# Decay matrices of a gated-delta layer: one symmetric matrix with masks applied later, in place of two masked ones

## The chip, the cores and the metric

The kernel runs on one core of a Trainium2 chip. The metric is the device time of one execution in microseconds. Engine names in the profile: PE is TensorE (matmuls; PEld its weight loads), DVE is VectorE, ACT is ScalarE, POOL is GpSimd, SP is SyncE, whose queue issues most loads; the ACT queue issues DMAs too. SBUF is the on-chip memory, PSUM the banks into which TensorE writes.

## What is computed

Two layers of a streaming encoder over 1024 prompt frames and 64 sample frames, 1024 features, in float32. The first layer (gated convolution and band attention) is not touched. The second is a gated DeltaNet with 8 heads of 128 keys and values, worked through in chunks of 64 frames. Cut to what matters here:

```python
gc = jnp.cumsum(g, axis=1)            # g <= 0: log decays, 64 frames of a chunk
decay = jnp.exp(jnp.where(incl, gct[..., :, None] - gct[..., None, :], -jnp.inf))
a = jnp.where(strict, bt[..., :, None] * kk * decay, 0.0)     # kk = k k^T
tmat = a + jnp.eye(L)
sol = lax.linalg.triangular_solve(tmat, rhs, left_side=True, lower=True, unit_diagonal=True)
qk = jnp.einsum('blhd,bmhd->bhlm', q, k) * decay
o = (q * exp(gc)) @ S + qk @ u
S_new = exp(g_last) * S + k_dec^T @ u
```

So for each chunk and head a 64 x 64 matrix exp(gc_i - gc_j) is needed twice: below the diagonal (i > j) for the triangular system, and with the diagonal, transposed, for the product of queries and keys.

## The kernel before, in words

**Order of the work.** TensorE's instructions are emitted in an order that `Order` (L75) keeps: generators yield the nanoseconds after which they want to go on, `mm` and `tr` (L115, L121) advance a clock by the estimated length of each matmul, and the free generator of the lowest rank goes next. Ranks: a scan 1, `solve` 1.3, `join` 1.5, `substitute` 1.6, `prepare` 2, the gates 2, the decays 3, and 5 for `main`, which is the stream of projections that fills what the others leave. The order on the other engines is made by the compiler's scheduler from what is ready in its own estimate of time; each engine then runs its queue in order.

**Layer two.** 17 chunks of 64 frames in batches of 6, 6 and 5 (`BATCHES`, L31); heads go in pairs, two heads by 64 rows on the 128 partitions, four pairs. `odd` (L670) first projects the keys and queries of pair 0 in three groups of frames (L1141 on), each with a short convolution on ScalarE and VectorE (`conv`, L701: an activation that evacuates the PSUM bank, L708, products with shifted copies, L721, and a tanh or SiLU, L724 to L727; pair 0 uses tanh). In the last group it adds `gates` (L779), which makes the sums gc and their exponentials, and `decays` (L819). Then come pair 0's values and the other pairs' keys, queries and values (L1165 on). Weights come through SP (L157) and are split into a high part by ScalarE (L163) and a low part by VectorE (L164).

**The decays before.** For each of four pairs and three batches: VectorE makes gx, a diagonal matrix of gc (L832); a matmul with a block of ones spreads it over the rows, into a PSUM bank with the tag `tr`; VectorE subtracts gc (L836) into an SBUF buffer df; GpSimd twice adds a mask of zeros and -1e30 (L839), each time into a buffer of its own; ScalarE takes the exponentials (L840) and the ACT queue stores each to DRAM (L841). All four buffers (gx, df, two results) are parts of `buf`, one of each. A name `dec{p}` is marked done after a pair's three batches.

**The batches.** `prepare` (L853) of a pair's batch waits for `dec{p}`, loads both matrices (L867, L868, SP queue, one buffer each), transposes keys and queries in `tr` banks, sums their squares on ScalarE (L882), makes reciprocal roots in small steps on VectorE (`rsqrt`, L683, its last step L690), scales the keys kt by kap on GpSimd (L894), and multiplies products of keys and queries in PSUM by scale and decay: An (L903) below the diagonal, KQD (L904) above it. Af (L907 to L910) gathers the 16-column blocks on An's diagonal; they go through DRAM to `substitute` (L916), which inverts them on GpSimd (L928, L929). `join` (L936) puts the inverse together, `solve` (L1004) applies it and `scan` (L1030) runs the recurrence. `add_pair` (L1124) names what each waits for: `prepare` of batch n for the one of n-1, the solve of n-2 and the scan of n-3. The tag `tr` has two PSUM banks for all of these (`pst`, L677).

Of the kernel before, what the change touches and what calls it, by code (L numbers as in the profile page):

```python
# [7 lines left out]
F32 = mybir.dt.float32  # L8
F32R = mybir.dt.float32r
I32 = mybir.dt.int32  # L10
AF = mybir.ActivationFunctionType
ALU = mybir.AluOpType
# [3 lines left out]
P = 128  # L16
# [8 lines left out]
NCH = T // 64  # L25
SCH = NCH - 1
EPS = 1e-6
NEG = -1.0e30
# [8 lines left out]

C_ID, C_U, C_BD = 0, 128, 256
C_ID64 = 384
C_M1, C_M2 = 448, 512  # L40
C_B16 = 576
C_H16 = 580
C_H = 582
# [13 lines left out]
def constants():  # L57
    c = np.zeros((P, NCONST), np.float32)
    p = np.arange(P)
    h, i = p // 64, p % 64  # L60
    same = h[:, None] == h[None, :]
    c[:, C_ID:C_ID + P] = np.eye(P)
    c[:, C_U:C_U + P] = same & (i[:, None] <= i[None, :])
    c[:, C_BD:C_BD + P] = same
    c[:, C_H:C_H + 2] = h[:, None] == np.arange(2)[None, :]
    j = np.arange(64)
    c[:, C_ID64:C_ID64 + 64] = i[:, None] == j[None, :]
    c[:, C_M1:C_M1 + 64] = np.where(j[None, :] < i[:, None], 0.0, NEG)
    c[:, C_M2:C_M2 + 64] = np.where(j[None, :] >= i[:, None], 0.0, NEG)
    c[:, C_B16:C_B16 + 4] = (i // 16)[:, None] == np.arange(4)[None, :]  # L70
    c[:, C_H16:C_H16 + 2] = (i // 16 % 2)[:, None] == np.arange(2)[None, :]
    return c
# [35 lines left out]
class Net:  # L108
# [120 lines left out]
    def run(self):  # L229
        nc, tc, I, O = self.nc, self.tc, self.I, self.O  # L230
        self.opened = {}
        const, self.wp, self.hp = self.open("const"), self.open("wp"), self.open("hp")
        dram = self.open("dram", space=DRAM)
        with tc.tile_pool(name="pj", bufs=2, space=PSUM) as self.pj:
            self.cst = const.tile([P, NCONST], F32, name="cst")
            self.par = const.tile([P, NPAR], F32, name="par")
            self.eps = const.tile([P, 1], F32, name="eps")
            self.cwa = const.tile([P, 12], F32, name="cwa")
            self.cwh = const.tile([P, 3, 8], F32, name="cwh")
            mean = const.tile([P, 1], F32, name="mean")  # L240
            self.dve.memset(mean, 1.0 / D)
            self.meanm = mean.broadcast_to([P, P])
            self.dve.memset(self.eps, EPS)
            self.ident = self.cst[:, C_ID:C_ID + P]
            self.mixd = [dram.tile([P, KT, T], F32, name=f"mixd{l}") for l in range(2)]
            self.od = dram.tile([P, KT, T], F32, name="od")
            self.xd = dram.tile([P, KT, T], F32, name="xd")
            self.Ld = dram.tile([8, LROW], F32, name="Ld")
            self.Gd = [dram.tile([P, LROW], F32, name=f"Gd{h}") for h in range(8)]
            self.Dd = [dram.tile([P, NCH, 64], F32, name=f"Dd{i}") for i in range(8)]  # L250
            self.Sd = [[dram.tile([m, P, 16], F32, name=f"Sd{a}{b}") for b, (c0, m) in enumerate(BATCHES)] for a in range(2)]
            self.H = [None] * len(GROUPS)
            self.ready, self.held = [], 0
            self.queue = []
            for p in range(4):
                self.queue += [I["w_in0"][i + p] for i in (24, 16, 20, 28, 4, 8, 12, 0)]
            self.queue += [I["w_out0"][m] for g in GROUPS for m in range(KT)]
            for p in range(4):
                self.queue += [I["w_in1"][i + 2 * p] for i in (8, 9, 0, 1, 16, 17)]
            self.queue += [I["w_in1"][24 + i] for i in range(8)]  # L260
            self.queue += [I["w_out1"][m] for g in GROUPS for m in range(KT)]
            self.banks, self.pg = [self.pj], None
            self.order.add("main", 5, self.main())
            self.order.run()
            self.close(*reversed([n for n in self.opened]))
# [404 lines left out]
    def odd(self):  # L670
        nc, tc, I, O = self.nc, self.tc, self.I, self.O
        act, dve, pool, par, cst = self.act, self.dve, self.pool, self.par, self.cst
        w_in, mix, order, Dd, od, Sd = I["w_in1"], self.mixd[1], self.order, self.Dd, self.od, self.Sd
# [3 lines left out]
        def pst(tag):  # L677
            return self.pg.tile([P, 512], F32, name=tag, tag=tag, bufs=2 if tag in ("tr", "su") else 1)
# [100 lines left out]
        def gates(ba):  # L779
# [36 lines left out]
            act.activation(egl.rearrange("p q a c -> p (q a c)"), ps[:, 136:272], AF.Exp)  # L816
            yield 1500

        def decays():  # L819
            gc = G["gc"]  # L820
            buf = G["buf"]

            def part(i, m):
                return buf[:, 384 * i:384 * i + 64 * m].rearrange("p (c j) -> p c j", j=64)

            for p in range(4):
                yield 0
                for c0, m in BATCHES:
                    sh = [P, m, 64]
                    gcb = gc[:, p, c0:c0 + m].unsqueeze(2).broadcast_to(sh)  # L830
                    gx, df = part(0, m), part(1, m)
                    dve.tensor_tensor(gx, gcb, cst[:, C_ID64:C_ID64 + 64].unsqueeze(1).broadcast_to(sh), ALU.mult)  # L832
                    yield 900
                    ps = pst("tr")
                    self.mm(ps[:, :64 * m], cst[:, C_BD:C_BD + P], gx.rearrange("p c j -> p (c j)"))
                    dve.tensor_tensor(df, ps[:, :64 * m].rearrange("p (c j) -> p c j", j=64), gcb, ALU.subtract)  # L836
                    for q, (cm, op) in enumerate(((C_M1, ALU.subtract), (C_M2, ALU.add))):
                        dx = part(2 + q, m)
                        pool.tensor_tensor(dx, cst[:, cm:cm + 64].unsqueeze(1).broadcast_to(sh), df, op)  # L839
                        act.activation(dx, dx, AF.Exp)  # L840
                        nc.scalar.dma_start(Dd[2 * p + q][:, c0:c0 + m, :], dx)  # L841
                    yield 2500
                order.done.add(f"dec{p}")

# [8 lines left out]
        def prepare(p, b):  # L853
            c0, nb = BATCHES[b]
            kq = KQ[p]
            n = NB * p + b
            yield 4000 if b == 0 else 0
            beta, egc, dec = G["beta"], G["egc"], G["dec"]

            def bt(name, w, bufs=1):  # L860
                return self.kp.tile([P, NBM, w], F32, name=name, tag=name, bufs=bufs)[:, :nb, :]
# [1 line left out]
            def small(name):  # L863
                return self.kp.tile([P, NBM], F32, name=name, tag=name, bufs=3)[:, :nb]

            Dst, DT = bt("Dst", 64), bt("DT", 64)
            nc.sync.dma_start(Dst, Dd[2 * p][:, c0:c0 + nb, :])  # L867
            nc.sync.dma_start(DT, Dd[2 * p + 1][:, c0:c0 + nb, :])  # L868
            kd, kt = bt("kd", P, 3), bt("kt", P, 2)
            ss = self.kp.tile([P, 2, NBM], F32, name="ss", tag="ss", bufs=2)[:, :, :nb]  # L870
            rr = self.kp.tile([P, 2, NBM], F32, name="rr", tag="rr", bufs=3)[:, :, :nb]
# [20 lines left out]
            dve.scalar_tensor_tensor(sA, sT, -1.0, rr[:, 0, :], ALU.mult, ALU.mult)  # L892
            dve.scalar_tensor_tensor(kap, egc[:, p, c0:c0 + nb], -1.0, rr[:, 0, :], ALU.mult, ALU.mult)
            pool.tensor_tensor(kt, kt, kap.unsqueeze(2).broadcast_to([P, nb, P]), ALU.mult)  # L894
            An, KQD = bt("An", 64, 2), bt("KQD", 64, 3)
            for i0 in range(0, nb, 4):
                m = min(4, nb - i0)
                ps = pst("tr").rearrange("p (c j) -> p c j", j=P)
                for i in range(m):
                    for q in range(2):  # L900
                        self.mm(ps[64 * q:64 * q + 64, i, :], kq[:, 0, c0 + i0 + i, q, :], kq[:, :, c0 + i0 + i, q, :], share=1.6)
                for i in range(m):
                    dve.scalar_tensor_tensor(An[:, i0 + i, :], ps[:, i, 0:64], sA[:, i0 + i:i0 + i + 1], Dst[:, i0 + i, :], ALU.mult, ALU.mult)  # L903
                dve.tensor_tensor(KQD[:, i0:i0 + m, :], ps[:, :m, 64:128], DT[:, i0:i0 + m, :], ALU.mult)  # L904
                yield 510

            Af = bt("Af", 16)  # L907
            dve.tensor_scalar(Af, An[:, :, 0:16], cst[:, C_B16:C_B16 + 1], None, ALU.mult)
            for j in range(1, 4):
                dve.scalar_tensor_tensor(Af, An[:, :, 16 * j:16 * j + 16], cst[:, C_B16 + j:C_B16 + j + 1], Af, ALU.mult, ALU.add)  # L910
            sa = Sd[0][b]
            nc.sync.dma_start(sa.rearrange("c r j -> r c j"), Af)
            R[p, b] = dict(kd=kd, kt=kt, KQD=KQD, rq=rr[:, 1, :], An=An, sT=sT)
# [210 lines left out]
        def add_pair(p):  # L1124
            for b in range(NB):
                n = NB * p + b
                def after(name, i):
                    return [f"{name}{i}"] if i >= 0 else []

                order.add(f"scan{n}", 1, scan(p, b), [f"wy{n}"] + after("scan", n - 1))  # L1130
                order.add(f"wy{n}", 1.3, solve(p, b), [f"inv{n}", f"v{p}"])
                order.add(f"inv{n}", 1.5, join(p, b), [f"sub{n}"] + after("wy", n - 1))
                order.add(f"sub{n}", 1.6, substitute(p, b), [f"prep{n}"] + after("sub", n - 1))
                order.add(f"prep{n}", 2, prepare(p, b), [f"dec{p}"] + after("prep", n - 1) + after("wy", n - 2) + after("scan", n - 3))

        new_kq(0)
        ba = k1.tile([P, 4 * T], F32, name="ba", tag="kq", bufs=2)[0:16, 0:T]
# [133 lines left out]
```

## Time and profile before

| | us |
|---|---|
| median of 3 runs | 1475.85 (1473.38 to 1477.38) |
| the profiled execution, its own time | 1476.87 |
| its span, first to last instruction | 1475.1 |
| mean granted TensorE clock | 0.980 |
| the twelve decay batches, first gx to last store issued | 714.1 to 797.2 |
| first state update to last of layer two | 815.5 to 1313.1 |

The profile is of one execution. Busy times are sums of instruction durations; matmul durations overlap. "Idle before" is an engine's idle time ahead of an instruction, put down to what released it last. A granted clock below 1 means that TensorE ran slower than its full rate in that window. A tile's name stands for all its buffers; `dbuf` is the `buf` of the gates and decays.

### The profile page before, as it was taken

What the parts mean: (1) busy time and instruction counts of PE and PEld (TensorE: products, weight loads), DVE (VectorE), ACT (ScalarE), POOL (GpSimd) and SP (SyncE); (2) the same over time, 40 slices, a digit from 0 to 9 for tenths busy, and PEclk for the clock granted to TensorE, in tenths of its full rate; (3) what the DMA queues carried; (4) which work ended last, traced back from release to release, by engine and by line L of the source; (5) the groups of instructions that cost most, each with busy time, mean ns of one, the idle gap of its engine ahead of it and who ended that gap; (6) DMA issues with size and microseconds to landing.
All of it is one profiled execution on the core that took longest, in us unless ns stands there. A gap on an engine that the chain in (4) does not pass through costs nothing. (4 is left out here: it accounts for less than half of the span.)

```text
span 1475.1 us, 28417 instructions
## 1 busy us (share of the span) xinstructions
PE 1371.8 (93%) x10578; PEld 1233.6 (84%) x10578; DVE 884.4 (60%) x2496; ACT 681.4 (46%) x1780; POOL 314.3 (21%) x813
## 2 busy tenths in 40 slices
PE   4999999999999999989878999999999989998995
PEld 3888998999899899878867777878887877888985
DVE  6647237425624855768687767666766656443654
ACT  6544144234424446775455553544443534323642
POOL 4100000000000012341136224240424152210332
PEclk9999999999999999999999999999999999999998
DMA  5231210211121164551432222122211232347454
GB/s 204 63 136 44 78 59 26 78 61 45 53 70 58 34 216 137 181 186 60 85 98 69 40 43 61 35 42 48 70 33 41 61 87 70 92 122 229 150 188 157
DMA packets 114378, 133.12 MB, mean 90 GB/s; under 512 B 35568, under 2 KB 81336, under 8 KB 114240
## 3 DMA queue, kind: packets, MB, share of 16 engines
q1 hardware_dynamic: 82128, 101.86, 24.2%
q10 hardware_dynamic: 32112, 29.45, 6.1%
q8 instruction: 83, 1.36, 0.4%
q14 instruction: 55, 0.45, 0.1%
HBM read 99.91 MB, written 34.51 MB: 91 GB/s over the span
## 5 line engine op out<-in xcount | busy, mean ns | idle before, releaser
L119 PE MATMUL pjt<-hhi,wlo 128*128 128x384 f32 (+1 forms) x1768 | 620.8, 351 | 2.5 <-DVE wlo L164 2.4
L119 PE MATMUL pjt<-hhi,whi 128*128 128x384 f32 (+1 forms) x1768 | 586.7, 332 | 19.5 <-ACT whi L163 4.1
L119 PE MATMUL pjt<-hlo,whi 128*128 128x384 f32 (+1 forms) x1768 | 585.9, 331 | 7.3 <-DVE hlo L217 6.6
L119 PEld LDWEIGHTS pjt<-hhi,whi 128*128 128x128 f32 x1768 | 339.5, 192 | 29.5 <-ACT hhi L216 6.6
L119 PEld LDWEIGHTS pjt<-hhi,wlo 128*128 128x128 f32 x1768 | 339.9, 192 | 27.5 <-issue 12.4
L119 PEld LDWEIGHTS pjt<-hlo,whi 128*128 128x128 f32 x1768 | 338.4, 191 | 10.5 <-DVE hlo L217 8.8
L164 DVE TENSOR_TENSOR wlo<-wf,whi 128x512 fp32r<-128x512 f32 x222 | 155.8, 727 | 144.7 <-ACT whi L163 143.0
L163 ACT CAST whi<-wf 128x512 fp32r<-128x512 f32 x222 | 130.0, 619 | 160.5 <-PE pjt L119 113.0
L546 ACT ACTIVATE pr<-pr,mx 128x640 f32<-128x640 f32 (+5 forms) x72 | 50.9, 707 | 92.7 <-DVE mx L545 92.2
L721 DVE SCALAR_TENSOR_TENSOR kq<-pjt,par,kq 128x384 f32<-128x384 f32 (+2 forms) x144 | 71.6, 497 | 2.9
L347 POOL TENSOR_TENSOR sqa<-sqa,sq 128x384 f32<-128x384 f32 (+1 forms) x36 | 37.9, 1052 | 154.0 <-ACT sq L345 153.9
L507 POOL MEMSET bias<- 64x64 f32 x8 | 1.4, 178 | 313.1 <-DMA bias<-Gd 312.6
L543 DVE CUSTOM_DVE_ANT_0 pr<-sc,bias 128x640 f32<-128x640 f32 (+5 forms) x72 | 48.0, 666 | 26.3 <-PE sc L119 22.8
L928 POOL TENSOR_TENSOR px<-AL 48x14 f32<-48x14 f32 (+6 forms) x168 | 45.1, 269 | 61.3 <-DMA AL<-Sd 52.2
L1091 DVE SCALAR_TENSOR_TENSOR S<-S,egl,su 128x128 f32<-128x128 f32 x128 | 40.6, 343 | 28.9 <-PE su L119 28.5
L692 POOL TENSOR_TENSOR so<-so 128x4 f32<-128x4 f32 (+2 forms) x72 | 16.8, 233 | 176.7 <-DVE so L685 117.9
L882 ACT ACTIVATE junk<-tr 128x128 f32<-128x128 f32 x136 | 37.7, 277 | 34.9 <-PE tr L124 29.5
L929 POOL TENSOR_TENSOR AL<-AL,px 48x14 f32<-48x14 f32 (+6 forms) x168 | 46.7, 278 | 9.4
L119 PE MATMUL pjt<-mhi,whi 128*128 128x384 f32 x128 | 43.9, 343 | 4.9 <-ACT mhi L163 4.9
L124 PE MATMUL pt<-cst,pr 128*128 128x128 f32 (+1 forms) x280 | 43.2, 269 | 4.4 <-DVE pr L548 2.9
L1050 ACT ACTIVATE junk<-o 128x128 f32<-128x128 f32 x68 | 21.0, 309 | 51.9 <-DVE o L1046 43.1
L119 PE MATMUL pjt<-mlo,whi 128*128 128x384 f32 x128 | 43.9, 343 | 0.0
(238 smaller groups left out, 2208.5 us busy)
## 6 DMA issues: line engine op xcount, KB each, us to landing
wf<-in_w_in SPq DMA_DIRECT2D x128, 256.0 KB, 3.3
wf<-in_w_out SPq DMA_DIRECT2D x96, 256.0 KB, 3.3
mf<-mixd SPq DMA_DIRECT2D x32, 192.0 KB, 3.2
x<-in_x SPq DMA_DIRECT2D x8, 384.0 KB, 5.4
xg<-in_x SPq DMA_DIRECT2D x2, 1536.0 KB
xd<-xg SPq DMA_DIRECT2D x2, 1536.0 KB, 6.9
Dd<-dbuf ACTq DMA_DIRECT2D x16, 192.0 KB, 2.7
od<-o ACTq DMA_DIRECT2D x12, 256.0 KB, 3.4
```

The source lines that it names most:

```text
L119: return self.pe.matmul(out, lhsT=lhsT, rhs=rhs, start=start, stop=stop, **k)
L124: return self.pe.transpose(out, in_, self.ident[0:k, 0:k])
L163: self.act.copy(out=hi, in_=x)
L164: (eng or self.dve).tensor_tensor(lo, x, hi.bitcast(F32), ALU.subtract)
L347: pool.tensor_tensor(acc, acc, sq, ALU.add)
L543: dve.tensor_tensor_reduce(out=cut(pr[0:nq, :nk]), in0=sc[0:nq, :nk // nw, :nw], in1=cut(b["bias"][a][0:nq, j0:j0 + nk]), scale=1.0, scala ...
L546: act.activation(pr[0:nq, :nk], pr[0:nq, :nk], AF.Exp, bias=mx[0:nq, 1:2], scale=1.0, accum_out=mx[0:nq, 2:3])
L721: dve.scalar_tensor_tensor(oi, ch(ps[:, i0 + j + 1:i0 + j + 1 + m]), cw[j], oi, ALU.mult, ALU.add)
L882: act.activation(junk, ps[:, i, :], AF.Square, accum_out=ss[:, a, i0 + i:i0 + i + 1])
L928: pool.tensor_tensor(t, AL[:, j + 1:16, j:j + 1].broadcast_to([lanes, m, w]), x.broadcast_to([lanes, m, w]), ALU.mult)
L929: pool.tensor_tensor(o, o, t, ALU.add)
L1091: dve.scalar_tensor_tensor(Sn[:, q, :], S[:, q, :], egl[:, q, p, c:c + 1], su[q], ALU.mult, ALU.add)
```

## The change

One exponential of minus the absolute difference, exp(-|gc_i - gc_j|), is symmetric; it is kept without a mask, as E. The masks become products later: the upper one (with the diagonal) is multiplied with E into KQD's buffer on GpSimd before KQD's product; the lower one isn't applied to An at all but, strict and inside the 16-column blocks only, to Af. The constants `C_M1` and `C_M2` become `C_LOW` (16 columns of ones below the diagonal of each block) and `C_UP`. The absolute value and the exponential both run on ScalarE, the first out of the PSUM bank, in which VectorE now subtracts in place.

`decays` does pairs 1 to 3 only, with two buffers for gx and three for E, and stores one matrix for each batch. Pair 0's decays are made inside `prepare`, straight into E, with An's buffer as scratch for gx; its batches no longer wait for `dec0` but for the gates. The 4000 ns ahead of a pair's first batch now come after the load or the decay.

```diff
@@ constants
-    c[:, C_M1:C_M1 + 64] = np.where(j[None, :] < i[:, None], 0.0, NEG)
-    c[:, C_M2:C_M2 + 64] = np.where(j[None, :] >= i[:, None], 0.0, NEG)
+    c[:, C_LOW:C_LOW + 16] = j[None, :16] < (i % 16)[:, None]
+    c[:, C_UP:C_UP + 64] = j[None, :] >= i[:, None]
@@ odd
+        def decay(e, gx, p, c0, m):
+            sh = [P, m, 64]
+            gcb = G["gc"][:, p, c0:c0 + m].unsqueeze(2).broadcast_to(sh)
+            dve.tensor_tensor(gx, gcb, cst[:, C_ID64:C_ID64 + 64].unsqueeze(1).broadcast_to(sh), ALU.mult)
+            yield 900
+            ps = pst("tr")[:, :64 * m]
+            self.mm(ps, cst[:, C_BD:C_BD + P], gx.rearrange("p c j -> p (c j)"))
+            ps = ps.rearrange("p (c j) -> p c j", j=64)
+            dve.tensor_tensor(ps, ps, gcb, ALU.subtract)
+            act.activation(e, ps, AF.Abs)
+            act.activation(e, e, AF.Exp, scale=-1.0)
...
-            for p in range(4):
-                yield 0
+            for p in range(1, 4):
                 for c0, m in BATCHES:
...
-                    dve.tensor_tensor(df, ps[:, :64 * m].rearrange("p (c j) -> p c j", j=64), gcb, ALU.subtract)
-                    for q, (cm, op) in enumerate(((C_M1, ALU.subtract), (C_M2, ALU.add))):
-                        dx = part(2 + q, m)
-                        pool.tensor_tensor(dx, cst[:, cm:cm + 64].unsqueeze(1).broadcast_to(sh), df, op)
-                        act.activation(dx, dx, AF.Exp)
-                        nc.scalar.dma_start(Dd[2 * p + q][:, c0:c0 + m, :], dx)
+                    e = piece(2 + i % 3, m)
+                    yield from decay(e, piece(i % 2, m), p, c0, m)
+                    nc.scalar.dma_start(Dd[p][:, c0:c0 + m, :], e)
+                    i += 1
                     yield 2500
@@ prepare
-            yield 4000 if b == 0 else 0
...
-            Dst, DT = bt("Dst", 64), bt("DT", 64)
-            nc.sync.dma_start(Dst, Dd[2 * p][:, c0:c0 + nb, :])
-            nc.sync.dma_start(DT, Dd[2 * p + 1][:, c0:c0 + nb, :])
+            E, An, KQD = bt("E", 64), bt("An", 64, 2), bt("KQD", 64, 3)
+            if p:
+                nc.sync.dma_start(E, Dd[p][:, c0:c0 + nb, :])
+            else:
+                yield from decay(E, An, p, c0, nb)
+            if b == 0:
+                yield 4000
...
             pool.tensor_tensor(kt, kt, kap.unsqueeze(2).broadcast_to([P, nb, P]), ALU.mult)
-            An, KQD = bt("An", 64, 2), bt("KQD", 64, 3)
+            pool.tensor_tensor(KQD, E, cst[:, C_UP:C_UP + 64].unsqueeze(1).broadcast_to([P, nb, 64]), ALU.mult)
...
-                    dve.scalar_tensor_tensor(An[:, i0 + i, :], ps[:, i, 0:64], sA[:, i0 + i:i0 + i + 1], Dst[:, i0 + i, :], ALU.mult, ALU.mult)
-                dve.tensor_tensor(KQD[:, i0:i0 + m, :], ps[:, :m, 64:128], DT[:, i0:i0 + m, :], ALU.mult)
+                    dve.scalar_tensor_tensor(An[:, i0 + i, :], ps[:, i, 0:64], sA[:, i0 + i:i0 + i + 1], E[:, i0 + i, :], ALU.mult, ALU.mult)
+                dve.tensor_tensor(KQD[:, i0:i0 + m, :], ps[:, :m, 64:128], KQD[:, i0:i0 + m, :], ALU.mult)
...
+            dve.tensor_tensor(Af, Af, cst[:, C_LOW:C_LOW + 16].unsqueeze(1).broadcast_to([P, nb, 16]), ALU.mult)
@@ add_pair
-                order.add(f"prep{n}", 2, prepare(p, b), [f"dec{p}"] + after("prep", n - 1) + after("wy", n - 2) + after("scan", n - 3))
+                order.add(f"prep{n}", 2, prepare(p, b), [f"dec{p}" if p else "gates"] + after("prep", n - 1) + after("wy", n - 2) + after("scan", n - 3))
```

More of the change, by code (lines that the diff above doesn't have):

```diff
@@ L39 @@
 C_ID64 = 384
-C_M1, C_M2 = 448, 512
+C_LOW, C_UP = 448, 512
 C_B16 = 576
@@ L249, in run @@
             self.Gd = [dram.tile([P, LROW], F32, name=f"Gd{h}") for h in range(8)]
-            self.Dd = [dram.tile([P, NCH, 64], F32, name=f"Dd{i}") for i in range(8)]
+            self.Dd = [dram.tile([P, NCH, 64], F32, name=f"Dd{i}") for i in range(4)]
             self.Sd = [[dram.tile([m, P, 16], F32, name=f"Sd{a}{b}") for b, (c0, m) in enumerate(BATCHES)] for a in range(2)]
@@ L817, in gates, with piece @@
             yield 1500
+        def decay(e, gx, p, c0, m):
[9 more added lines that the diff above has]
+            act.activation(e, e, AF.Exp, scale=-1.0)
         def decays():
-            gc = G["gc"]
-            buf = G["buf"]
-            def part(i, m):
+            buf, i = G["buf"], 0
+            def piece(i, m):
                 return buf[:, 384 * i:384 * i + 64 * m].rearrange("p (c j) -> p c j", j=64)
-            for p in range(4):
-                yield 0
+            for p in range(1, 4):
                 for c0, m in BATCHES:
[L829 to L836, printed above, removed]
-                    for q, (cm, op) in enumerate(((C_M1, ALU.subtract), (C_M2, ALU.add))):
-                        dx = part(2 + q, m)
-                        pool.tensor_tensor(dx, cst[:, cm:cm + 64].unsqueeze(1).broadcast_to(sh), df, op)
-                        act.activation(dx, dx, AF.Exp)
-                        nc.scalar.dma_start(Dd[2 * p + q][:, c0:c0 + m, :], dx)
+                    e = piece(2 + i % 3, m)
+                    yield from decay(e, piece(i % 2, m), p, c0, m)
+                    nc.scalar.dma_start(Dd[p][:, c0:c0 + m, :], e)
+                    i += 1
                     yield 2500
```

## Prediction

> **What bounds the kernel now.** I began with the page's first part and then asked the view by windows for the stages around the change (columns: window, its length, then busy time and instruction count of PE, PEld, DVE, ACT and POOL, granted clock, DMA share, GB/s).
>
> ```profile
> PE 1371.8 (93%) x10578; PEld 1233.6 (84%) x10578; DVE 884.4 (60%) x2496; ACT 681.4 (46%) x1780; POOL 314.3 (21%) x813
> ```
>
> ```profile
> 713.00:800.00 87.00, 69.92 (x454) 61.14 (x456) 69.56 (x178) 43.90 (x122) 39.86 (x67) 0.90 0.39 96
> 800.00:1240.00 440.00, 418.75 (x4323) 350.81 (x4310) 297.38 (x1091) 202.07 (x698) 137.94 (x531) 0.98 0.23 52
> 1240.00:1334.00 94.00, 93.51 (x753) 80.52 (x754) 40.45 (x140) 30.38 (x89) 23.73 (x99) 1.00 0.34 101
> 1334.00:1475.00 141.00, 117.12 (x659) 111.10 (x658) 73.74 (x110) 63.71 (x129) 33.18 (x30) 0.93 0.57 185
> ```
>
> TensorE is the bound: busy 93% of the span, and without a gap from 1240 to 1334. Its work is not touched (the same twelve decay matmuls), so time can only come out of its idle stretches and low clock. The decays are all computed between 713 and 800 us. There TensorE idles 87.00 - 69.92 = 17.1 us, works at a mean clock of 0.90 (about 0.10 x 69.92 = 7.0 us more), and VectorE is busy 80%. Everything later runs at its own pace behind this stretch. TensorE's waits in it name who is late (us in total, times, longest):
>
> ```profile
> PE tr L119 <- DVE KQD L904: 4.3, 1, 4.3
> PE tr L124 <- DVE KQD L904: 3.6, 1, 3.6
> PE tr L124 <- DVE dbuf L836: 3.0, 2, 1.6
> PE pjt L119 <- ACT vt L708: 2.6, 1, 2.6
> PE tr L119 <- ACT junk L882: 1.7, 2, 1.1
> PE tr L119 <- DVE dbuf L832: 1.3, 2, 1.0
> ```
>
> VectorE holds 4.3 + 3.6 + 3.0 + 1.3 = 12.2 us of them, ScalarE 2.6 + 1.7. Three causes can be seen in the timeline (start, duration, engine; in brackets the idle time before and its releaser).
>
> ```profile
> 728.25 1.96 POOL L839 TENSOR_TENSOR dbuf<-cst,dbuf 128x384 f32<-128x384 f32 x2 [9.22 <-DMA Dd<-dbuf]
> 729.30 0.52 ACT L840 ACTIVATE dbuf<-dbuf 128x384 f32<-128x384 f32 x1 [7.86 <-POOL dbuf L839]
> 731.18 0.58 ACT L708 ACTIVATE vt<-pjt,cwh 128x384 f32<-128x384 f32 x1 [0.41 <-ACT dbuf L840]
> 731.88 0.38 PE L119 MATMUL pjt<-hhi,whi 128*128 128x320 f32 x1 [2.57 <-ACT vt L708]
> 734.75 0.47 PE L119 MATMUL pjt<-hlo,whi 128*128 128x320 f32 x1
> 736.11 0.31 PE L119 MATMUL pjt<-hlo,whi 128*128 128x320 f32 x1
> ```
>
> First: GpSimd's masking (L839) of the second batch waits 9.22 us for the store of the first batch's result, whose buffer is single; ScalarE's exponential waits 7.86 us behind it, the V tile's evacuation (L708) behind that, and TensorE loses 2.57 us. After the wait a 320-column matmul takes 0.47 us instead of 0.31: the lost clock costs again.
>
> ```profile
> 780.72 2.30 DVE L690 SCALAR_TENSOR_TENSOR rr<-rt,rr 128x12 f32<-128x12 f32 x1
> 780.80 0.98 POOL L839 TENSOR_TENSOR dbuf<-cst,dbuf 128x384 f32<-128x384 f32 x1
> 782.00 0.98 POOL L839 TENSOR_TENSOR dbuf<-cst,dbuf 128x384 f32<-128x384 f32 x1
> 784.43 0.28 POOL L929 TENSOR_TENSOR AL<-AL,px 48x50 f32<-48x50 f32 x1
> 784.67 1.46 POOL L894 TENSOR_TENSOR kt<-kt,kap 128x768 f32<-128x768 f32 x1
> 785.09 0.41 DVE L904 TENSOR_TENSOR KQD<-tr,DT 128x256 f32<-128x256 f32 x1
> 785.65 1.62 PE L119 MATMUL tr<-dbuf,cst 128*128 128x384 f32 x2 [4.33 <-DVE KQD L904]
> 786.10 0.28 POOL L928 TENSOR_TENSOR px<-AL 48x44 f32<-48x44 f32 x1
> ```
>
> Second: a twelve-column step of the reciprocal root (L690) takes 2.30 us while GpSimd runs two masks, and what follows it (KQD, L904) releases TensorE 4.33 us late. The groups by form show how general that is, the three first rows in 713 to 800, the next three the same forms in 860 to 1240, where no decays run, then the decays' own operations (busy us, mean ns).
>
> ```profile
> L164 DVE TENSOR_TENSOR wlo<-wf,whi 128x512 fp32r<-128x512 f32 x8 | 7.2, 927 | 1.2 <-ACT whi L163 1.2
> L910 DVE SCALAR_TENSOR_TENSOR Af<-An,cst,Af 128x96 f32<-128x96 f32 x6 | 4.0, 668 | 0.0
> L690 DVE SCALAR_TENSOR_TENSOR rr<-rt,rr 128x12 f32<-128x12 f32 x6 | 3.9, 652 | 0.2
> ...
> L164 DVE TENSOR_TENSOR wlo<-wf,whi 128x512 fp32r<-128x512 f32 x32 | 21.6, 690 | 8.5 <-ACT whi L163 8.1 <-PE pjt L119 0.3
> L910 DVE SCALAR_TENSOR_TENSOR Af<-An,cst,Af 128x96 f32<-128x96 f32 x18 | 6.9, 384 | 0.1
> L690 DVE SCALAR_TENSOR_TENSOR rr<-rt,rr 128x12 f32<-128x12 f32 x18 | 3.4, 187 | 0.3
> ...
> L836 DVE TENSOR_TENSOR dbuf<-tr,gc 128x384 f32<-128x384 f32 x8 | 4.4, 555 | 3.4 <-PE tr L119 2.2 <-POOL dbuf L839 1.1
> L839 POOL TENSOR_TENSOR dbuf<-cst,dbuf 128x384 f32<-128x384 f32 x16 | 18.2, 1153 | 63.2 <-DVE dbuf L836 53.9 <-DMA Dd<-dbuf 9.2
> L839 POOL TENSOR_TENSOR dbuf<-cst,dbuf 128x320 f32<-128x320 f32 x8 | 8.5, 1074 | 13.2 <-DVE dbuf L836 7.8 <-ACT whi L163 3.4 <-ACT th L724 2.1
> L840 ACT ACTIVATE dbuf<-dbuf 128x384 f32<-128x384 f32 x16 | 8.4, 525 | 16.7 <-POOL dbuf L839 15.6 <-ACT th L724 1.0
> ```
>
> These three forms alone lost 8 x 0.237 + 6 x 0.284 + 6 x 0.465 = 6.4 us of VectorE. Third: L836, which must release its PSUM bank (3.0 us of waits), simply stands in VectorE's full queue.
>
> **The change, part by part.**
>
> *Masks leave the decays.* All 24 L839 go: 18.2 + 8.5 = 26.7 us of GpSimd, two thirds of its 39.9 in the stretch. Each batch gets one mask product on GpSimd (E times the upper mask into KQD), 1.15 us by the same rows; in this stretch two or three, 3 us. I credit VectorE with two thirds of the 6.4 us, 4.3, and put it all on the path, because 12.2 of these 16.5 us of waits are on VectorE: -4.3 (bounds 0, if other queued work takes the place, and -12.2).
>
> [...]
>
> *Three buffers, one product.* Stores fall from 24 to 9, loads likewise, and a piece's buffer is used again only three batches later: the 9.22 us wait goes, and with it TensorE's 2.6 (bounds 0 and -2.6). Next in line behind it is ScalarE's own wait for the difference from VectorE; I take that as covered by the shorter chain, since the two masks between difference and exponential (2 x 1.15 us) are gone. If that cover fails, the 2.6 us stay.
>
> *Clock.* 7.0 us of lost clock over 16.5 us of waits is 0.42 us for each: 0.42 x (4.3 + 2.6) = -2.9 (bounds 0 and -7.0).
>
> *Absolute value on ScalarE.* An exponential (525 ns) becomes an absolute value read from PSUM (0.58 us by L708); ScalarE has 43 us idle in the stretch, so its sum costs nothing. But the bank, free after L836 until now, stays taken for that activation too. TensorE waited for L836 twice in twelve decays: 2 x 0.58 = +1.2 (bounds: 0, where the other bank is free; 12 x 0.58 plus a queue, the third rival). The difference now writes PSUM in place; the nearest row is L836 itself, so I take 0, with 0.1 us for each of twelve as my own margin either way.
>
> *First pair on chip.* Its three decays move into the batches: the same two VectorE and two ScalarE operations, no stores, no loads. The first batch can start once the gates are done instead of after three decay batches; the other pairs' decays lose three places in the queue. The third batch's decays now lie behind the first batch's solve (its scratch is An), one difference, absolute value and exponential longer (0.55 + 0.58 + 0.53 = 1.7 us, plus a matmul); the cover is projections of the second pair, which keep TensorE at 95% after 800. I take 0 (bounds -2 and +2).
>
> *Lower mask in the 16-column blocks.* One more VectorE operation for each batch, 0.38 us by L910: 12 x 0.38 = 4.6 us, two of them in the full stretch. +0.3 (bounds 0 and 0.8).
>
> *The twelve mask products elsewhere.* After 800 GpSimd is busy 31%; +1.0 (bounds 0 and the fourth rival).
>
> Tables of ScalarE are reloaded in this stretch where the second pair's SiLU meets the last exponentials:
>
> ```profile
> L727 ACT ACT_TABLE_LOAD x3 | 3.8, 1283 | 0.5 <-ACT dbuf L840 0.4
> L840 ACT ACT_TABLE_LOAD x2 | 2.6, 1283 | 0.0
> ```
>
> Nine instead of twelve queued decays should end before that SiLU, so some of these 6.4 us go; nothing on TensorE waits for them here, so 0 (bounds 0 and -1.7).
>
> Sum: -4.3 - 2.6 - 2.9 + 1.2 + 0.3 + 1.0 = -7.3 us. The profiled execution took 1476.87 us (span 1475.1), so it would take 1469.6. It lies 1.0 above the median of the three runs, 1475.85; against the median that is **1468.6 us**.
>
> **Rivals.**
>
> *Full relief.* All waits on VectorE and the 2.6 go with their clock: -(12.2 + 2.6) x 1.42 + 2.5 = -18.5, 1457.4. For it: L690's 2.30 us. Against: VectorE still has 69.6 - 6.4 = 63 us of work in these 87, and the 4.33 us wait held a serial chain of small steps of which only 2.1 us were lost to GpSimd.
>
> *Hidden anyway.* VectorE stays the late one because the batches of the first pair now start earlier, on top of the V tiles: what leaves is filled again. Only the 2.6 us go, and the added operations take them back: 1475. For it: VectorE 80% busy.
>
> *Banks held by the absolute value (slower).* Two banks serve decays, transposes and products. Each decay now holds one until ScalarE, in its own order, gets to it: 0.58 plus a cast or tanh ahead of it (about 0.5, the size of L840), 1.1 us x 12 x 1.42 = 18.7 against the 9.8 gained: +8.9, 1484.8. It decides from 9.8 / (12 x 1.42) = 0.58 us of added wait for each decay. Against it: only two of twelve waited before.
>
> *Mask product behind the kt product (slower).* If GpSimd runs it in the written order, KQD comes later:
>
> ```profile
> 834.72 1.26 POOL L894 TENSOR_TENSOR kt<-kt,kap 128x640 f32<-128x640 f32 x1
> 835.50 0.41 DVE L904 TENSOR_TENSOR KQD<-tr,DT 128x256 f32<-128x256 f32 x1
> 837.37 0.68 PE L119 MATMUL tr<-BD,kt 128*128 128x128 f32 x4 [0.24 <-DVE KQD L904]
> ```
>
> L894 ends at 835.98, a 1.07 us mask at 837.05, and L904 slips 1.55 us; TensorE, which waits 0.24 here, would wait about 1 more, 12 x 1.0 - 7.3 = +4.7, 1480.6. Against: the mask needs only E, which is asked for before the batch's transposes, not kap; and GpSimd's order is not that of the batches (at 784.67 L894 stands between two steps, L929 and L928, of another batch's substitution).
>
> *Absolute value outside the loaded set.* Two loads for each decay: 24 x 1.283 = 30.8 us of ScalarE, half of it on the path, 15.4 - 7.3 = +8.1, 1484. [...] No absolute value is in this trace.
>
> **How the numbers follow.** Forecast 0.50, full relief 0.12, hidden 0.18, banks 0.11, mask order 0.06, tables 0.03. A change within 0.3% (4.4 us) is about what a measurement of this kernel cannot tell from none. Nine tenths of the forecast and all of full relief lie beyond it: faster 0.45 + 0.01 + 0.12 = 0.58 (the hundredth from the favourable end of hidden). Same: the rest of the forecast, most of hidden and a third of mask order, 0.24. Slower: 0.18. The range runs from just below full relief, 1456, to just past mask order, 1481; it leaves out the banks, the tables and a little at the low end. The forecast's own range is 1463 to 1474.
>
> **What would show it.** Right: no 9 us wait of GpSimd for a store before 728; L690 and L910 back at 0.19 and 0.38 us; idle of TensorE in the 90 us after the gates down from 17 to about 10 and its clock above 0.93; 9 stores and 9 loads; KQD's mask ahead of the kt product. Wrong: a wait of TensorE's transposes or decays for the absolute value of over 0.5 us each; waits for KQD above 800 growing from the few tenths each; reloads beside every decay; or the first stretch relieved and as much idle time turning up between 800 and 1240.

## The result and the profile after

The changed kernel took 1492.56 us (median of 4 runs, 1491.90 to 1493.98), the kernel before beside it 1475.78: ratio 1.0122, 95% interval [1.0104, 1.0141]. Ratios here and below are to the kernel before as it ran beside each kernel, as recorded; they differ by up to 0.2% from the quotients of the medians, here 1.0114. The forecast was 1468.6 with a range to 1481. It is slower, by 17 us between the medians and 18 by the ratio, and outside the range.

The profiled execution has a span of 1492.2 us (1475.1 before). The first part of its page, and the windows that were read before the change:

```profile
PE 1376.3 (92%) x10578; PEld 1236.8 (83%) x10578; DVE 875.7 (59%) x2508; ACT 681.1 (46%) x1778; POOL 299.7 (20%) x801
```

```profile
713.00:800.00 87.00, 76.62 (x587) 69.03 (x586) 66.74 (x203) 44.25 (x131) 22.75 (x64) 0.92 0.23 61
800.00:1240.00 440.00, 403.29 (x3969) 336.89 (x3967) 287.58 (x1044) 198.73 (x670) 136.63 (x516) 0.97 0.19 46
1240.00:1334.00 94.00, 93.46 (x915) 77.53 (x914) 47.25 (x180) 31.96 (x101) 24.37 (x99) 1.00 0.30 88
```

VectorE, ScalarE and GpSimd all have no more to do than before, and TensorE does the same 10578 matmuls. In the first window TensorE's idle time fell from 17.1 to 87.00 - 76.62 = 10.4 us, almost as forecast. In the second it rose from 21.3 to 440.00 - 403.29 = 36.7 us, and its clock fell from 0.98 to 0.97. Over the whole span TensorE idles 1492.2 - 1376.3 = 115.9 us against 103.3 (+12.6), and is busy 4.5 us longer at the lower clock (0.973 against 0.980): together the 17.1 us of the span.

First the part that came true. TensorE's waits between 713 and 800 us, then groups by form in that window (busy us, mean ns):

```profile
PE tr L119 <- DVE KQD L909: 4.1, 2, 3.4
PE tr L119 <- issue: 2.6, 1, 2.6
PE tr L119 <- ACT dbuf L829: 1.3, 1, 1.3
PE tr L119 <- DVE dbuf L823: 1.1, 1, 1.1
PE tr L124 <- ACT dbuf L829: 0.8, 1, 0.8
```

```profile
L164 DVE TENSOR_TENSOR wlo<-wf,whi 128x512 fp32r<-128x512 f32 x11 | 7.6, 700 | 1.4 <-ACT whi L163 1.4
L915 DVE SCALAR_TENSOR_TENSOR Af<-An,cst,Af 128x96 f32<-128x96 f32 x6 | 1.9, 314 | 0.0
L690 DVE SCALAR_TENSOR_TENSOR rr<-rt,rr 128x12 f32<-128x12 f32 x6 | 1.0, 165 | 0.1
```

With the 24 masks gone, L690 takes 165 ns instead of 652, the gathering step (L910, now L915) 314 instead of 668, L164 700 instead of 927. The bank waits for the absolute value are 1.3 + 0.8 = 2.1 us in two places; 1.2 had been set. The wait for the V tile behind GpSimd and the store (2.6 us) is gone. Table loads in 700 to 815 us:

```profile
L727 ACT ACT_TABLE_LOAD x2 | 2.6, 1283 | 0.0
L799 ACT ACT_TABLE_LOAD x1 | 1.3, 1283 | 0.0
L812 ACT ACT_TABLE_LOAD x1 | 1.3, 1283 | 0.0
L830 ACT ACT_TABLE_LOAD x1 | 1.3, 1283 | 0.0
```

None is at the absolute value, L829.

Now the part that did not. TensorE's waits between 800 and 1340 us, after the change and then before it (us in total, times, longest):

```profile
PE tr L124 <- DVE o L1118: 23.7, 5, 9.0
PE tr L119 <- ACT vt L1031: 5.1, 3, 3.0
PE tr L119 <- DVE KQD L909: 3.4, 8, 1.1
```

```profile
PE tr L124 <- DVE o L1112: 4.6, 2, 3.3
PE su L119 <- DVE us L1077: 4.0, 3, 2.7
...
PE tr L119 <- DVE KQD L904: 1.3, 5, 0.3
```

One wait has grown from 4.6 to 23.7 us, and the change does not touch its line: the transposes of the outputs o in `finish`, the step that normalises up to four chunks' outputs and sends them out. The large ones stand where one pair gives way to the next: 9.01 us at 915.49, 6.90 at 1062.27, 5.30 at 1208.74; 1.99 at 1336.94 is the end of the last pair. The first in the timeline (start, duration, engine; idle before and its releaser):

```profile
894.67 0.29 DVE L1052 TENSOR_TENSOR o<-tr,qs 128x128 f32<-128x128 f32 x1
...
903.14 0.28 ACT L887 ACTIVATE junk<-tr 128x128 f32<-128x128 f32 x1 [1.45 <-PE tr L124]
904.18 0.21 POOL L934 TENSOR_TENSOR px<-AL 48x14 f32<-48x14 f32 x1 [6.64 <-DMA AL<-Sd]
904.21 0.31 ACT L1056 ACTIVATE junk<-o 128x128 f32<-128x128 f32 x1
905.39 1.09 PE L119 MATMUL tr<-kq 128*64 128x128 f32 x16
907.77 0.19 POOL L692 TENSOR_TENSOR so<-so 128x4 f32<-128x4 f32 x1
910.67 1.47 POOL L899 TENSOR_TENSOR kt<-kt,kap 128x768 f32<-128x768 f32 x1
914.86 0.16 DVE L1116 SCALAR_TENSOR_TENSOR so<-so,rr 128x4 f32<-128x4 f32 x1 [4.43 <-POOL so L695]
915.06 1.02 DVE L1118 TENSOR_SCALAR o<-o,so 128x128 f32<-128x128 f32 x4
915.49 1.16 PE L124 MATMUL tr<-cst,o 128*128 128x128 f32 x4 [9.01 <-DVE o L1118]
916.30 0.62 PE L119 MATMUL pjt<-hhi,wlo 128*128 128x320 f32 x1
```

The last of the four outputs is made at 894.67. Its square (L1056) runs on ScalarE at 904.21, behind squares of keys and queries of the next pair's second batch (L887), which themselves wait for TensorE. The reciprocal root (L692 to L695) runs on GpSimd between the steps of the next pair's substitution (L934, L935), which started late for its data, and a kt product. TensorE comes to the transposes at 906.5 and stands there for 9.01 us; a projection right behind them in its queue, which needs nothing of all this, starts only at 916.30.

Right behind the three large waits, in 915 to 918 us, 1062 to 1066 and 1209 to 1213, the granted clock is 0.50 each time; in the kernel before, in the same stretches, 0.50, 1.00 and 1.00. The 50 us around the first, after the change and then before it:

```profile
900.00:950.00 50.00, 39.49 (x380) 35.24 (x378) 29.43 (x101) 17.68 (x55) 21.62 (x88) 0.90 0.17 40
```

```profile
900.00:950.00 50.00, 47.31 (x540) 40.61 (x536) 33.71 (x118) 21.45 (x72) 20.82 (x83) 0.93 0.25 53
```

### The profile page after: what moved, and what is told of

Its sections match the earlier page's. It is cut to its first block, busy times and chain, and to the rows that moved or that the text cites. A ratio compares the mean times of both kernels' runs of the same rounds, so it can differ in the third digit from the quotient of the medians.

```text
span 1492.2 us, 28339 instructions
## 1 busy us (share of the span) xinstructions
PE 1376.3 (92%) x10578; PEld 1236.8 (83%) x10578; DVE 875.7 (59%) x2508; ACT 681.1 (46%) x1778; POOL 299.7 (20%) x801
## 5 line engine op out<-in xcount | busy, mean ns | idle before, releaser
L164 DVE TENSOR_TENSOR wlo<-wf,whi 128x512 fp32r<-128x512 f32 x222 | 152.7, 714 | 154.5 <-ACT whi L163 152.9
L934 POOL TENSOR_TENSOR px<-AL 48x14 f32<-48x14 f32 (+6 forms) x168 | 45.3, 269 | 60.5 <-DMA AL<-Sd 51.0
L887 ACT ACTIVATE junk<-tr 128x128 f32<-128x128 f32 x136 | 37.8, 278 | 30.8 <-PE tr L124 27.5
L1056 ACT ACTIVATE junk<-o 128x128 f32<-128x128 f32 x68 | 21.0, 310 | 63.6 <-DVE o L1052 46.1
L935 POOL TENSOR_TENSOR AL<-AL,px 48x14 f32<-48x14 f32 (+6 forms) x168 | 47.0, 280 | 9.6
L692 POOL TENSOR_TENSOR so<-so 128x4 f32<-128x4 f32 (+2 forms) x72 | 14.8, 206 | 163.6 <-DVE so L685 158.9
```

What stands on the lines that cost most here:

```text
L164: (eng or self.dve).tensor_tensor(lo, x, hi.bitcast(F32), ALU.subtract)
L887: act.activation(junk, ps[:, i, :], AF.Square, accum_out=ss[:, a, i0 + i:i0 + i + 1])
L934: pool.tensor_tensor(t, AL[:, j + 1:16, j:j + 1].broadcast_to([lanes, m, w]), x.broadcast_to([lanes, m, w]), ALU.mult)
L935: pool.tensor_tensor(o, o, t, ALU.add)
```

## The experiments

In the expectations and here, *the order* is TensorE's hand-kept order. `Order`'s own clock (planned ns, no measured time) shows how it moved. Where the first pair waits for the decays, as before, the plan ends its boundary steps thus: third pair-0 batch solved, then second batch of pair 1 prepared (prep4), its first substitution (sub3), then the last scan of pair 0 (scan2) and its finishing step (fin0.2.0). In the changed kernel pair 0 is planned some 8 us earlier (solve of its first batch done at 667.0 instead of 675.2 planned us), and scan2 and fin0.2.0 go ahead of prep4 and sub3. At the next two boundaries the plan hardly differs: of the steps of these kinds that end there, only the neighbours prep6 and scan5 change places. The theory: this shift, caused by starting pair 0 from the gates, loses the time. The rivals: the added mask products lose it, or the absolute value's hold of the banks.

**First pair later.** The changed kernel, pair 0 still on chip, but starting only when pair 1's decays are done.

```diff
-[f"dec{p}" if p else "gates"]
+[f"dec{max(p, 1)}"]
```

> The changed kernel whole, but the first pair's batches wait for three decay batches (those of the second pair), as they did before the change. Its TensorE order after 800 us is then again that of the kernel before. Theory (the order: by starting early, the first pair's batches moved the hand-written order so that each pair's last finishing step meets the next pair's substitution in GpSimd's queue): the waits of TensorE for the finished outputs (DVE o) fall from 23.7 us to about 5, and the time to 1475 or less, about 1470. Rival (the operations: GpSimd's twelve mask products and the longer way from An to the substitution): those waits stay near 20 us, 1488 to 1493.

Measured 1463.59 us (the kernel before beside it 1471.56), 0.9936 [0.9912, 0.9959]. TensorE's windows, and its first waits from 800 to 1340:

```profile
713.00:800.00 87.00, 82.31 (x638) 74.40 (x637) 69.97 (x215) 47.92 (x138) 20.46 (x61) 0.98 0.24 61
800.00:1340.00 540.00, 512.00 (x4989) 430.76 (x4988) 340.08 (x1231) 236.78 (x789) 167.10 (x624) 0.98 0.25 67
```

```profile
PE pjt L119 <- ACT mhi L163: 5.8, 1, 5.8
PE tr L124 <- DVE o L1118: 5.6, 2, 4.6
PE tr L119 <- ACT E L829: 5.4, 1, 5.4
```

The wait for o is back at 5.6 us, and the kernel with every added operation in it is faster than before. One string in a list of names is worth 1.0122 - 0.9936 = 1.9%.

**All four pairs stored.** Pair 0's decays go through the generator and DRAM as before.

```diff
-            for p in range(1, 4):
+            for p in range(4):
...
-            if p:
-                nc.sync.dma_start(E, Dd[p][:, c0:c0 + nb, :])
-            else:
-                yield from decay(E, An, p, c0, nb)
+            nc.sync.dma_start(E, Dd[p][:, c0:c0 + nb, :])
...
-[f"dec{p}" if p else "gates"]
+[f"dec{p}"]
```

> The changed kernel, but all four pairs' decays go through the decay generator and DRAM; one exponential, three buffers and the later masks stay. Order after 800 us as in the kernel before. Theory (order): 1470 to 1476, waits for DVE o about 5 us. Rival (operations): 1488 to 1493, as all of them are still there.

Measured 1468.40, 0.9963 [0.9944, 0.9982]; the wait for o, put at about 5 us, is 8.2. So the masks moved into the batches, one exponential and three buffers are a gain without the first pair's part.

**The early start without the new arithmetic.** The kernel before, with its two masked exponentials, pair 0's made inside `prepare` and its start taken from the gates; the 4000 ns stand behind the load or the decay, as in the changed kernel.

```diff
-            for p in range(4):
+            for p in range(1, 4):
...
+            if p:
                 nc.sync.dma_start(Dst, Dd[2 * p][:, c0:c0 + nb, :])
                 nc.sync.dma_start(DT, Dd[2 * p + 1][:, c0:c0 + nb, :])
+            else:
...
+                for dx, cm, op in ((Dst, C_M1, ALU.subtract), (DT, C_M2, ALU.add)):
+                    pool.tensor_tensor(dx, cst[:, cm:cm + 64].unsqueeze(1).broadcast_to(sh), DT, op)
+                    act.activation(dx, dx, AF.Exp)
...
-[f"dec{p}"]
+[f"dec{p}" if p else "gates"]
```

> The kernel before with one part of the change alone: the first pair's decays are made in its batches, with both additive masks and two exponentials as before, and its batches wait for the gates only. TensorE's order is that of the changed kernel. Theory (order): slow as well, 1488 to 1496, with waits for DVE o of about 20 us. Rival (operations): about as before, 1472 to 1478, since no mask product is on GpSimd after 800 us and Af has no added step.

Measured 1499.95, 1.0175 [1.0138, 1.0212], 4 us above the range that was expected. Its planned steps are the changed kernel's, and its wait for o is nearly so:

```profile
PE tr L124 <- DVE o L1124: 21.9, 4, 9.5
PE tr L119 <- ACT vr L1028: 5.4, 2, 4.9
PE tr L119 <- DVE KQD L916: 3.4, 8, 1.1
```

This is the loss with nothing of the new arithmetic. The run moves pair 0's decays on chip as well as its start, so by itself it doesn't tell these two apart; the run with pair 0 later, which keeps them on chip, does.

**No masks at all.** The changed kernel without KQD's mask product and without the lower mask of Af.

```diff
-            pool.tensor_tensor(KQD, E, cst[:, C_UP:C_UP + 64].unsqueeze(1).broadcast_to([P, nb, 64]), ALU.mult)
...
-                dve.tensor_tensor(KQD[:, i0:i0 + m, :], ps[:, :m, 64:128], KQD[:, i0:i0 + m, :], ALU.mult)
+                dve.tensor_tensor(KQD[:, i0:i0 + m, :], ps[:, :m, 64:128], E[:, i0:i0 + m, :], ALU.mult)
...
-            dve.tensor_tensor(Af, Af, cst[:, C_LOW:C_LOW + 16].unsqueeze(1).broadcast_to([P, nb, 16]), ALU.mult)
```

> The changed kernel without both later masks: neither GpSimd's mask product for KQD nor VectorE's lower mask on Af is done (the decays stay unmasked). TensorE's order is that of the changed kernel. Theory (order): hardly faster, ratio to the kernel before 1.008 to 1.013. Rival (the added operations cost the time after 800 us): 0.993 to 1.002.

Measured 1489.54, 1.0110 [1.0058, 1.0162]:

```profile
PE tr L124 <- DVE o L1116: 20.6, 5, 8.2
PE tr L119 <- ACT vt L1029: 6.8, 3, 4.6
PE tr L119 <- ACT E L829: 3.4, 1, 3.4
PE tr L119 <- DVE KQD L908: 3.4, 8, 1.1
```

The added products are not the loss; even the waits for KQD, 3.4 us in 8, stay without the product ahead of it.

**Shorten or postpone the finishing step.** Four runs on the changed kernel ask whether the wait for o itself is the loss. All four came out slower than their theories put them. First the root on VectorE:

```diff
-            rsqrt(fa, va, tm, pool)
+            rsqrt(fa, va, tm, dve)
```

> The changed kernel with the reciprocal root of the finishing step on VectorE instead of GpSimd, so it cannot queue behind the substitution there. Theory (GpSimd's in-order queue between finishing and substitution): waits of TensorE for DVE o vanish, 1492.6 - (23.7 - 2) x 1.2 to 1.4 = 1462 to 1468, less some VectorE time. Rival (the finishing step is late for another reason, its own chain on VectorE or a late scan): the waits stay over 12 us and the time within 5 us of 1492.

Measured 1485.44, 1.0080 [1.0050, 1.0109]; wait for o 15.6 us. Then the squares as well, with an output tile of their own (`junk`, which nothing reads):

```diff
-                act.activation(junk, o4[:, a, :], AF.Square, accum_out=so[:, 0, a:a + 1])
+                dve.tensor_tensor_reduce(out=junk, in0=o4[:, a, :], in1=o4[:, a, :], scale=1.0, scalar=0.0, op0=ALU.mult, op1=ALU.add, accum_out=so[:, 0, a:a + 1])
```

> The changed kernel with the finishing step wholly on VectorE: the sums of squares of the outputs (on ScalarE until now) and their reciprocal root (on GpSimd). TensorE's order is unchanged. Theory, now narrower (in the changed order the outputs' squares stand in ScalarE's queue behind eight squares of the next pair's second batch, and their root in GpSimd's behind the substitution): with both gone the waits for DVE o fall from 23.7 us, and 15.6 with the root alone on VectorE, to under 8; ratio to the kernel before 0.997 to 1.005. Rival (VectorE's own queue holds the finishing step): waits of 12 us or more, ratio 1.008 or more.

Measured 1483.66, 1.0055 [1.0030, 1.0079]; wait for o 10.3, but 5.9 for XT and more small ones. Then a longer planned time:

```diff
-            yield 9000
+            yield 15000
```

> The changed kernel; only the planned time between a finishing step's start and its transposes on TensorE is 15 us instead of 9, so that they stand later in TensorE's order. Theory (the early start brings the finishing step of one pair behind the next pair's first batches in VectorE's and GpSimd's queues, and TensorE, whose order allows it 9 us, waits at its transposes): waits for DVE o fall from 23.7 us to under 8, ratio to the kernel before about 1.000 (0.994 to 1.004). Rival (the later stages lose their time all over, to the added operations): ratio stays 1.008 or more.

Measured 1483.37, 1.0057 [1.0030, 1.0083]; wait for o 17.3. Then the next pair's second batch held back until the old pair's finishing step is in:

```diff
-                order.add(f"prep{n}", 2, prepare(p, b), [f"dec{p}" if p else "gates"] + after("prep", n - 1) + after("wy", n - 2) + after("scan", n - 3))
+                order.add(f"prep{n}", 2, prepare(p, b), [f"dec{p}" if p else "gates"] + after("prep", n - 1) + after("wy", n - 2) + after("scan", n - 3) + ([f"fin{p - 1}.{NB - 1}.0"] if p and b == 1 else []))
```

> The changed kernel; a pair's second batch is only prepared after the last full group of outputs of the pair before is finished, so its squares no longer stand ahead of the finishing step. Theory: waits for DVE o under 8 us, ratio to the kernel before 0.996 to 1.005 (the later second batch may cost a few us of its own). Rival (any shift of the order costs): 1.008 or more with other waits in their place.

Measured 1487.63, 1.0091 [1.0059, 1.0123], its runs 1477.57 to 1497.05; the profiled one, with a span of 1475.7 and a wait for o of 5.7, is the shortest of the ten (ratio 1.0024), so what the longer ones waited for isn't known. The waits for o in the four runs:

```profile
PE tr L124 <- DVE o L1118: 15.6, 4, 6.4
PE tr L124 <- DVE o L1118: 10.3, 3, 8.4
PE tr L124 <- DVE o L1118: 17.3, 4, 5.9
PE tr L124 <- DVE o L1118: 5.7, 3, 2.7
```

Of the 1.86% between the changed kernel and the run with pair 0 later, the four give back 0.42, 0.67, 0.65 and 0.31. The wait for o fell by 8.1, 13.4, 6.4 and 18.0 us, which is 0.55, 0.91, 0.43 and 1.22% of 1475 us. So in the first three, as far as one profiled run of each can say, it is worth about its own length, within the intervals; in the fourth much less, and no profile shows why. TensorE's other idle time between 800 and 1340 is 15.5 us in the changed kernel, 15.7 and 14.7 in the first and third of the four, and about 20 in the second and fourth: only in these two did a part of the wait turn up elsewhere. The same 15000 was given to the run with pair 0 later and to the kernel before, as controls.

> Both remedies: the first pair's batches wait for the second pair's decays, and the finishing step is allowed 15 us. Theory: the waits for DVE o left in the first remedy (5.6 us) fall below 2; ratio to the kernel before 0.990 to 0.994. If the later transposes hold back the end instead, 0.994 to 1.000.

> The kernel before with the finishing step allowed 15 us. Theory: it waits for DVE o 4.6 us only, so there is little to gain: ratio 0.996 to 1.001. Rival (a longer allowance is worth 10 us or more in any order, so that it says nothing on the change): 0.993 or less.

Measured 1476.29, 1.0013 [0.9988, 1.0038], and 1484.54, 1.0073 [1.0049, 1.0097]: each 0.7 to 0.8% slower than the same kernel with 9000, where a small gain and hardly any change had been expected. A later finishing step is thus no good in itself: the same number helps one plan and hurts the other two.

**Only the pause.** The changed kernel whole, with the start from the gates; only the planned pause ahead of pair 0's first batch is longer.

```diff
-                yield 4000
+                yield 4000 if p else 6000     # 8000, 10000, 16000
```

> The changed kernel whole, its first pair still started from the gates; only the planned pause ahead of that pair's first batch is 6000 instead of 4000 ns. In TensorE's planned order the old pair's finishing step (fin0.2.0) now stands behind the second batch's preparation (prep4) and the substitution (sub3), its last scan (scan2) still ahead of them. Theory (the order at the pair boundary loses the time): part of the loss goes, 1.002 to 1.009 of the kernel before, waits for the outputs o after 800 us between 8 and 18 us (23.7 in the changed kernel). Rival (the first pair beside the queued decays loses it, whatever the order): 1.010 to 1.014, waits unchanged.

> As before, pause 8000 ns. The planned order has prep4, scan2, sub3, fin0.2.0: the second batch's preparation ahead of the last scan, as in the kernel before the change, the substitution still behind it. Theory: most of the loss goes, 0.993 to 1.002, waits for o under 12 us. Rival: 1.008 to 1.014.

> Pause 10000 ns. The planned order after the first pair is now that of the run in which the first pair waits for dec1 (prep3, prep4, sub3, scan2, fin0.2.0), which took 0.9936. Theory: 0.991 to 0.997, waits for o under 9 us, TensorE busy over 509 us between 800 and 1340. Rival: 1.007 to 1.014, since the first pair's decays still run beside the queued ones.

> Pause 16000 ns: later than in any kernel so far; planned order sub3, prep4, scan2, inv3, fin0.2.0. If a later start only helped by the order, this new order has no reason to beat 10000 and its planned end of the first pair is 5 us later: 0.993 to 1.006. If a late start as such is what helps (the rival, more distance from the decays), it is at or under the 10000 run, below 0.993.

| pause, ns | ratio | profiled run, ratio | wait for o, 800 to 1340 | TensorE busy, 800 to 1340 |
|---|---|---|---|---|
| 4000 | 1.0122 [1.0104, 1.0141] | 1.0123 | 23.7 | 500.8 |
| 6000 | 1.0107 [1.0083, 1.0131] | 1.0131 | 17.9 | 497.7 |
| 8000 | 1.0057 [1.0034, 1.0079] | 1.0113 | 12.2 | 500.6 |
| 10000 | 1.0007 [0.9994, 1.0021] | 1.0005 | 8.1 | 508.8 |
| 16000 | 1.0111 [1.0095, 1.0126] | 1.0105 | 10.9 | 500.6 |

The two last columns are of the profiled run; the one with 8000 was the longest of its seven, so its row shows more loss than its ratio.

The window from 800 to 1340 of the run with 10000, then of the one with 16000:

```profile
800.00:1340.00 540.00, 508.82 (x4948) 426.95 (x4948) 339.12 (x1229) 233.54 (x781) 170.46 (x633) 0.97 0.24 57
```

```profile
800.00:1340.00 540.00, 500.58 (x4875) 416.54 (x4875) 334.15 (x1224) 231.20 (x776) 167.26 (x643) 0.97 0.22 53
```

The first step gained nothing that can be told from 4000, and its ratio lies in the rival's bounds, though the wait for o did fall; 8000 and 10000 lie between theory and rival; 16000, put at 0.993 to 1.006, is as slow as 4000. So the forecast from the list of planned steps was too simple: the step by which prep4 passes scan2 does not bring the whole gain. But the rival, all four near 1.012 because the first pair's decays run beside the queued ones, is refuted. With the same instructions the time falls by 1.15% as the pause goes from 4000 to 10000, although the first two on-chip absolute values still run among the nine queued ones (at 729.3 and 756.0 us with 4000, 729.7 and 763.3 with 10000). It comes back at 16000, where the second one, at 768.8, is behind them all. So this part of the loss hangs on where pair 0's steps fall in the order, and a late start as such does not help. At 16000 the wait for o is 10.9 of 540 - 500.58 = 39.4 us idle; no other group of waits is over 3.2. There the loss is spread over many small waits.

**Third batch through DRAM.** The run with pair 0 later has a 5.4 us wait for a bank that its third batch's on-chip absolute value (E, L829) sets free; the expectation below names the exponential, which is L830. VectorE subtracts in that bank at 806.03, and the absolute value follows at 806.59. Here that batch alone is stored and loaded.

```diff
-            for p in range(1, 4):
-                for c0, m in BATCHES:
+            for p in (1, 0, 2, 3):
+                for c0, m in BATCHES if p else BATCHES[2:]:
...
-            if p:
+            if p or b == 2:
...
-[f"dec{p}" if p else "gates"]
+[f"dec{p}" if p or b == 2 else "dec1"]
```

> The first remedy (first pair's batches after the second pair's decays), and the first pair's third batch takes its decays through DRAM again, so only two batches are made on chip. In the first remedy TensorE waits 5.4 us once for the third batch's exponential, which comes after the solve with a table reload. Theory (that batch is dear on chip): the wait goes, 4 to 7 us less than the first remedy, ratio to the kernel before 0.989 to 0.992. Rival (the wait hides another, or VectorE's stretch before 800 us pays for it): 0.993 to 0.997.

Measured 1466.10, 0.9929 [0.9906, 0.9952]. The wait is gone, and the time, at the rival's lower bound, is the same as without this edit, within the intervals: 2.9 us more of waits for the scaled outputs (8.5) and another 2.6 for the substitution stand in its place. These two are the best versions, 0.6 to 0.7% under the kernel before.

## Why the prediction was wrong

*First pair on chip* is the step that failed: "I take 0 (bounds -2 and +2)". It saw that "the first batch can start once the gates are done", took this for a small good, and priced only the third batch's decay chain, which came to one wait of 0.8 us (for E, L829). In the changed kernel the early start alone, one name in a list, costs 1.9%, 27 us; in the kernel before, the early start together with the decays on chip costs 1.75% [1.38, 2.12], 0.0175 x 1475.85 = 25.8 us. The cover named for it, projections of the second pair, does keep TensorE busy around 800 us (46.54 of the 50 us from 800 to 850); it does not help at 906, where projections stand behind the waiting transposes in the same queue. The step treated TensorE's order as fixed. It is made from planned times, and a pair that starts 8 us earlier on that clock changes which steps stand ahead of which at the first pair boundary, while the other engines' queues are filled in their own order. The front part of the document describes both orders; the sum had no term for them.

The other steps:

- *Masks leave the decays* (-4.3) was right in kind: the three forms that were slow beside the masks are back near their quiet lengths, at the counts of before worth 8 x 0.227 + 6 x 0.354 + 6 x 0.487 = 6.9 us of VectorE, of which 4.3 had been credited, the author's estimate. TensorE's idle time in the stretch fell 6.7 us where the terms of the sum without the clock and the twelve products make -4.3 - 2.6 + 1.2 + 0.3 = -5.4; no run takes the masks away alone, so this term's own share isn't known. Where pair 0 waits for dec1 more idle time went (82.31 us busy of 87). The subtraction, which reads a bank, took 555 ns beside the masks (L836) and 559 without them (L828, into the bank); why the three forms were slow there and the subtraction was not is not shown.
- *Three buffers, one product* (-2.6): no wait of GpSimd for a store is left in the stretch (9.2 us before), and TensorE no longer waits for the V tile there.
- *Clock* (-2.9): in the stretch it rose only from 0.90 to 0.92, not above 0.93; 0.08 x 76.6 = 6.1 us are still lost against 7.0. A low clock right behind single long waits is in the traces (0.50 above), but a loss in proportion to all waits, 0.42 us for each, is not borne out: without the later masks TensorE idles 87.00 - 73.72 = 13.3 us in the stretch at a clock of 0.98, in the changed kernel 10.4 us at 0.92. The size of this term rested on one trace.
- *Absolute value on ScalarE* (+1.2): 2.1 us of waits in the stretch, 1.3 and 0.8; each is over the 0.5 us set as a sign of being wrong, but there are only two. No table load was added: 18 of 1283 ns in the whole execution against 20 before, none at L829, which ran twelve times; the rival on tables is out.
- *Lower mask* (+0.3) and *the twelve mask products* (+1.0): without both the ratio is 1.0110 [1.0058, 1.0162], not to be told from 1.0122. The mask did run ahead of the kt product, the first at 730.40 us against 749.26; the slower rival of that name did not happen.
- *Hidden anyway* had half of the cause ("the batches of the first pair now start earlier"), but put it into the first stretch, at no loss. The stop sign that the prediction set up itself, "the first stretch relieved and as much idle time turning up between 800 and 1240", is what came, with 15.4 us more idle there against 6.7 less.

Without the early start the total comes out: 0.9936 x 1475.85 = 1466.4 us with pair 0 on chip, 0.9963 x 1475.85 = 1470.4 with it stored, around the forecast of 1468.6. The terms were not measured one by one, and the clock's was not borne out, so that the total is so near is in part luck.

What is shown: the moment at which pair 0 starts in the plan loses the time, by one dependency in the changed kernel, and 1.15 of the 1.86% come and go with a planned pause alone. What stays open: which displaced step costs how much. In the profiles the waits for o make 23.7 - 5.6 = 18.1 of the 27 us, but they were never taken away alone: the pause of 10000 took 15.6 of them and gave back 1.15%, 17 us; the runs that work on the finishing step gave back at most 0.67%, 10 us. The plan shifts at the first boundary, where 9.0 of the 23.7 us stand; why the wait also grows at the next two, where the plan hardly differs, was not settled. Why a 10000 ns pause, whose planned steps after pair 0 are those of the best version, is 0.7% slower than it, was not settled; its wait for E is longer (8.8 us against 5.4), but taking that wait away from the best version gained nothing.

## What to carry to other kernels

When a change lets a step start earlier, it is an edit of the order, whatever its operations cost. In a kernel whose busiest engine runs a planned queue in order, look up what then moves ahead of what in that queue, and which chain on the other engines must be finished when the moved step comes to its head. Measure the start separately from the arithmetic: here the kernel without the early start was 0.4 to 0.7% under the one before, the early start cost 1.75 to 1.9%, and one dependency kept the first without the second.

## What the runs showed that was not expected

With the same instructions, nothing but a planned pause moved the time between 1.0007 and 1.0122, and not in one direction. VectorE's small steps recovered wholly, not by two thirds, when GpSimd's masks left: L690 from 652 to 165 ns, below the 187 of the quiet stretch before. And runs of one kernel can lie far apart: with the second batch held back, 1477.57 to 1497.05 us.
